# Conditioning dots laid out anew, one section of them moved to the end, and norms from sums and squares

## The chip, the cores and the metric

The kernel runs on one core of a Trainium2 chip. The core has a matrix engine (TensorE, PE in the profile; its weight loads are PEld), three engines for elementwise work (VectorE = DVE, ScalarE = ACT, GpSimd = POOL), a sequencer that mostly issues transfers (SyncE = SP), and 16 DMA engines. Each engine works through its own instructions in order and waits on semaphores for the others. The metric is the device time of one launch in microseconds, as the median of several runs.

## The reference

One layer of a diffusion backbone: 512 latent tokens `x` and 256 context tokens `ctx`, 1024 channels each. Only the latent stream is returned.

```python
mod_x = (jax.nn.silu(c) @ w_ada + b_ada).reshape(bsz, N_MOD, 1, d)      # N_MOD = 9
mod_c = (jax.nn.silu(c_ctx) @ w_ada + b_ada).reshape(N_MOD, 1, d)
...
def ffn_sublayer(h, m, i, w_up, w_down):
    shift, scale, gate = sub_mod(m, i)                                  # m[3i], m[3i+1], m[3i+2]
    y = swiglu(modulate(h, shift, scale), w_up, w_down)
    return post_ln(DEEPNORM_ALPHA * h + 0.5 * gate * y, ln_g[i], ln_b[i])

x = ffn_sublayer(x, mod_x, 0, ffn1_w_in, ffn1_w_out)                    # first network
ctx = ffn_sublayer(ctx, mod_c, 0, ffn1_w_in, ffn1_w_out)
... # projections, neighbourhood attention, gated delta rule, merge
x = ffn_sublayer(x, mod_x, 2, ffn2_w_in, ffn2_w_out)                    # second network
```

`modulate` is a layer norm followed by scale and shift; `post_ln` is a layer norm with gain and bias. The width of both networks is 2816, which is 22 blocks of 128. `mod_x` has nine sections of 1024 values, counted 0 to 8; section 8 is the gate of the second network, section 2 that of the first, and the context needs only sections 0 to 4.

## The kernel before

**Matmuls.** Float32 products are made of three faster ones. Each weight tile of 128x1024 is loaded raw (tags `wr`, `ra`, `rb`, 512 KB), then split: ACT casts the high half `wh` (L137), DVE subtracts to get the low half `wl` (L139). PE multiplies high by high, low by high and high by low (L192 to L194 for the up products and projections, L211 for the down products). The activations are split the same way (`uxh` and `uxl` for x, `uch` and `ucl` for the context, `hx` and `hc` for the hidden blocks). So each weight passes SP (the load), ACT and DVE before PE can use it, and each of these queues is in order.

**Stages up to 600 us.** (1) The x loop, f = 0 to 7: eight of the 22 hidden blocks for the x tokens, one up unit each (512-column matmuls). (2) The c loop, the same eight blocks for the context (256 columns). (3) `t_sums`: DVE forms sums of activation quarters for the next stage while PE runs the down product of these eight blocks. (4) Fourteen `Seven` units, the other 14 blocks for x and context together, in seven products of 384 columns. (5) `bx`, the down product of these 14 for x, four token tiles; (6) `hc`, the same for the context, two tiles; (7) the projections. Between 600 and 1394 us lie the mixers and the second network's up product, and from 1394 us its down product (called dn2 here).

**The evacuation and the norms.** While `bx` ends, `evac1` (L629 to L634) multiplies each finished bank by the gate and adds the residual (`ax`, 512 columns at a time). `finish1` (L636 on) does two layer norms per tile: `post_ln` (L258, L259), then the norm of the following modulate, whose result `y` is made on ACT. The statistics are two `bn_stats` and a `bn_aggr` on DVE, then `rsqrt_eps` (an addition, and a power on POOL, L114). `to_u` then transposes `y` on PE (L148), ACT scales and shifts it into `u32` (L151, one buffer of 1024 columns), and a split gives `uxh` and `uxl`. This runs for x tile by tile inside `hc`, at its steps 0, 2, 5 and 8, and the projections wait for the last tile.

**The conditioning dots.** `w_ada` is held transposed, 72 tiles of 128x1024. A dot (`dot_cols`, L280) is one DVE operation: tile times the broadcast silu row, with the sum of the product as its second output, one column of `colx` (or of `colc` for the context). `ada_gen` (L290 to L304) walks sections 2 to 8, one tile per step: one load on SP, and one dot, or two in sections 2 to 4. `ada_step(n)` takes n steps of it; the steps are spread over the stages by constants: two behind the x loop, one in each of the first six units of the c loop, one per step of `t_sums`, `ADA2` for the Seven units, `ADA3` for `bx`. A few loops take raw buffers for the dots from those of the weights (`raw1`: five in turn); in `bx` there are two of their own.

**What sets the order.** The code is recorded, and a scheduler with its own costs then lays out each engine's order; `issue_after` holds an instruction behind a mark. The order is fixed when the program is built.

Of the kernel before, what the change touches and what calls it, by code (L numbers as in the profile page):

```python
# [58 lines left out]
def body(ctx, tc, I, out, dbg=None):  # L59
# [96 lines left out]
    class Stream:  # L156
# [120 lines left out]
    def dot_cols(tp, raw, crow, col, c):  # L277

        pr = tl(tp, [P, D], "adap")
        V.scalar_tensor_tensor(pr[:], raw[:], 1.0, crow, op0=ALU.mult, op1=ALU.mult, accum_out=col[:, c:c + 1])  # L280
# [104 lines left out]
    ADA2 = (2,) * 10 + (1, 1, 1, 0)  # L385
    ADA3 = (3, 3, 3, 3, 3, 3, 2, 2)
# [74 lines left out]
    ada_step(2)  # L461
# [14 lines left out]
    for f in range(N1):  # L476
        hc.append(h_c())
        ffn_unit(tp, pp, ws.get(), ws.get(), uch, ucl, NCT, *hc[-1])
        ada_step(f < 6)
    rows_out(tp, "fs", 2)  # L480
    accd = tl(dp, [6, P, D], "accd")

    def t_sums(j):
# [3 lines left out]
        ada_step()  # L487
# [133 lines left out]
    for t in range(4):  # L621
        nc.gpsimd.dma_start(accx[t][:], accd[t])
# [6 lines left out]
    def evac1(p, banks, acc, out, g):  # L629
        for d in range(2):  # L630
# [3 lines left out]
            V.tensor_tensor(out[:, sl], h[:], acc[:, sl], ALU.add)  # L634
# [61 lines left out]
    for t in range(4):  # L696
        evac1(lp, bx[t], accx[t], accx[t], gx)
# [1173 lines left out]
```

## Time and profile before

| | |
|---|---|
| median of 3 runs | 1523.51 us (1523.34 to 1525.52) |
| the profiled execution | 1524.35 us, span 1522.6 us, mean granted PE clock 0.984 |
| busy share | PE 95%, DVE 76%, ACT 43%, POOL 14% |
| bytes moved | 248.03 MB, mean 163 GB/s |

The span runs from the first to the last instruction. In a row of the timeline stand start, duration, engine, line, operation, output and inputs, the count, and in brackets the idle time just before with what ended it. In a row of waits stand engine and tile and line, the releaser, total us, times, longest. In a row of groups: busy time and mean ns, then idle time before them and its releasers. In a row of windows: the window, its length, then busy time and count of PE, PEld, DVE, ACT and POOL, the granted PE clock, the DMA share and GB/s.

### The profile page before, as it was taken

To read this page: it belongs to the slowest core of one execution; us is meant where nothing else is said; L and a number is where in the kernel's file an instruction comes from. 1 tells how busy PE (TensorE), PEld (TensorE's weight loads), DVE (VectorE), ACT (ScalarE), POOL (GpSimd) and SP (SyncE) were. 2 spreads that over 40 slices of the span, in tenths; PEclk is the share of its full clock that TensorE was granted. 3 is DMA by queue.
4 is the path that set the end of the run, shared out by engine and by line. 5 is a ranking of instruction groups with operands and counts; after the bars stand their busy time and mean duration, and the time that the engine had idled before them with its cause. 6 is when DMAs were issued, how large, how long until landed. Compare 5 with 4: busy or idle time off the path is not lost.

```text
span 1522.6 us, 23874 instructions
## 1 busy us (share of the span) xinstructions
PE 1442.9 (95%) x9118; PEld 1265.1 (83%) x9118; DVE 1161.1 (76%) x1992; ACT 648.8 (43%) x1067; POOL 209.6 (14%) x251
## 2 busy tenths in 40 slices
PE   6999999999999988999996999989999999999997
PEld 4779879999997776889875777867778999998886
DVE  8768888999977895768777796567669799886426
ACT  5434424434334165546533444266516444444310
POOL 0000000000010020323301001333232022220001
PEclk9999999999999998999998999999999999999999
DMA  9666775445459643222476623274354143233422
GB/s 371 204 234 225 237 250 208 163 161 200 161 214 344 235 161 119 91 90 85 145 216 171 192 79 122 70 253 139 100 177 139 65 135 111 94 111 139 138 84 83
DMA packets 114756, 248.03 MB, mean 163 GB/s; under 512 B 35073, under 2 KB 50513, under 8 KB 114641
## 3 DMA queue, kind: packets, MB, share of 16 engines
q1 hardware_dynamic: 109632, 227.30, 44.5%
q0 software_dynamic: 3424, 13.90, 2.4%
q10 hardware_dynamic: 1586, 5.32, 0.9%
q8 instruction: 71, 1.16, 0.3%
q14 instruction: 43, 0.35, 0.1%
HBM read 214.98 MB, written 31.50 MB: 162 GB/s over the span
## 4 chain that ended last, share of the span: by engine, by line
PE 65%; DVE 13%; DMA 12%; issue 4%; ACT 3%; POOL 2%; SPq 1%; DVEq 0%; ACTq 0%; POOLq 0%
PE ps L211 12%; PE ps L531 4%; PE ps L530 4%; PE ps L532 4%; PE pm L192 4%; PE pm L193 4%; PE pm L194 4%; PE ps L1659 3%; PE ps L1658 3%; PE ps L1660 3%; DVE wl L139 3%; DMA wr<-in_w_adaT_dram 3%; PE ps L194 3%; PE ps L193 3%; PE ps L192 3%
## 5 line engine op out<-in xcount | busy, mean ns | idle before, releaser
L139 DVE TENSOR_TENSOR wl<-wr,wh 128x1024 fp32r<-128x1024 f32 (+1 forms) x183 | 224.0, 1228 | 115.2 <-ACT wh L137 114.8
L137 ACT CAST wh<-wr 128x1024 fp32r<-128x1024 f32 (+1 forms) x183 | 184.4, 1012 | 292.8 <-PE pm L193 60.3
L192 PE MATMUL pm<-uxh,wh 128*128 128x512 f32 x320 | 132.7, 415 | 1.1 <-ACT spill L777 1.0
L194 PE MATMUL pm<-uxh,wl 128*128 128x512 f32 x320 | 126.9, 397 | 0.7 <-DVE wl L139 0.7
L193 PE MATMUL pm<-uxl,wh 128*128 128x512 f32 x320 | 126.9, 397 | 0.0
L280 DVE SCALAR_TENSOR_TENSOR adap<-wr,crow 128x1024 f32<-128x1024 f32 x92 | 112.1, 1219 | 13.9 <-DMA wr<-in_w_adaT_dram 13.2
L211 PE MATMUL ps<-wh,hx 128*128 128x512 f32 x352 | 97.3, 395 | 4.1 <-ACT wh L137 4.1
L114 POOL TENSOR_TENSOR rs<-ve,mhalf 128x1 f32<-128x1 f32 (+2 forms) x46 | 51.2, 1118 | 327.5 <-DVE ve L110 326.2
L211 PEld LDWEIGHTS ps<-wh,hx 128*128 128x128 f32 x352 | 66.7, 190 | 18.8 <-ACT wh L137 5.0
L194 PEld LDWEIGHTS pm<-uxh,wl 128*128 128x128 f32 x320 | 61.0, 191 | 14.7 <-DVE wl L139 1.6
L192 PEld LDWEIGHTS pm<-uxh,wh 128*128 128x128 f32 x320 | 61.2, 191 | 12.9 <-ACT spill L777 1.9
L192 PE MATMUL ps<-uh,wh 128*128 128x256 f32 (+1 forms) x208 | 68.6, 330 | 2.0 <-ACT wh L137 2.0
L194 PE MATMUL ps<-uh,wl 128*128 128x256 f32 (+1 forms) x208 | 67.6, 327 | 3.0 <-DVE wl L139 3.0
L193 PEld LDWEIGHTS pm<-uxl,wh 128*128 128x128 f32 x320 | 61.4, 192 | 10.5
L192 PE MATMUL ps<-uxh,wh 128*128 128x256 f32 (+1 forms) x192 | 60.6, 324 | 9.6 <-ACT uxh L137 9.6
L193 PE MATMUL ps<-ul,wh 128*128 128x256 f32 (+1 forms) x208 | 67.7, 326 | 0.0
L137 ACT CAST wh<-ra 128x1024 fp32r<-128x1024 f32 x32 | 33.7, 1052 | 75.1 <-issue 16.9
L193 PE MATMUL ps<-uxl,wh 128*128 128x256 f32 (+1 forms) x192 | 61.1, 320 | 1.0 <-DVE uxl L139 0.9
L194 PE MATMUL ps<-uxh,wl 128*128 128x256 f32 (+1 forms) x192 | 60.6, 318 | 0.0
L530 PE MATMUL ps<-ur,wh 128*128 128x384 f32 x168 | 56.5, 336 | 0.0
L531 PE MATMUL ps<-ur,wh 128*128 128x384 f32 x168 | 56.4, 336 | 0.0
L530 PE MATMUL ps<-uh,wh 128*128 128x384 f32 x168 | 56.4, 336 | 0.0
(483 smaller groups left out, 4217.3 us busy)
## 6 DMA issues: line engine op xcount, KB each, us to landing
wr<-in_w_adaT_dram SPq DMA_DIRECT2D x72, 512.0 KB, 4.6
wr<-in_up_dram SPq DMA_DIRECT2D x54, 512.0 KB, 3.4
wr<-in_dn_dram SPq DMA_DIRECT2D x52, 512.0 KB, 3.5
wr<-in_win_dram SPq DMA_DIRECT2D x52, 512.0 KB, 3.5
ra<-in_up_dram SPq DMA_DIRECT2D x26, 512.0 KB, 4.1
rb<-in_up_dram SPq DMA_DIRECT2D x18, 512.0 KB, 3.3
ra<-in_w_adaT_dram SPq DMA_DIRECT2D x16, 512.0 KB, 4.4
wr<-in_w_o_dram SPq DMA_DIRECT2D x8, 512.0 KB, 4.0
```

Of the source, the lines that this page charges most:

```text
L114: G.tensor_tensor(rs[:], ve[:], mhalf[:, 0:n], ALU.pow)
L137: S.copy(hi, src)
L139: marks["lo"] = V.tensor_tensor(lo, src, hi.bitcast(F32), ALU.subtract).ins
L192: T.matmul(ps, a, uh[:, k, :], start=(k == 0), stop=False)
L193: T.matmul(ps, a, ul[:, k, :], start=False, stop=False)
L194: marks["mm"] = T.matmul(ps, b, uh[:, k, :], start=False, stop=(k == nk - 1)).ins
L211: T.matmul(banks[t][d][:, c0:c1], a[:, sl], b[:, d * 512 + c0:d * 512 + c1], start=first and j == 0, stop=last and j == 2)
L280: V.scalar_tensor_tensor(pr[:], raw[:], 1.0, crow, op0=ALU.mult, op1=ALU.mult, accum_out=col[:, c:c + 1])
L530: T.matmul(ps[:], a, mh, start=k == 0, stop=False)
L531: T.matmul(ps[:], a, ml, start=False, stop=False)
L532: T.matmul(ps[:], b, mh, start=False, stop=k == 3)
L1658: T.matmul(ps[:], a, uh[:, k], start=k == 0, stop=False)
```

## The change

It does three things. First, section 8 leaves `ada_gen` (48 steps are left of 56): its eight loads and dots stand in dn2, one at each of the steps j = 5 to 12, in place in the raw tile; the silu row is written to DRAM at the start (`sild`) and broadcast back at j = 4 (`arow`); at j = 13 bias and factor 0.5 are put on, and POOL's queue writes the gate (1024 single values) and broadcasts it into `gx`, which was loaded at dn2's start before. Second, the remaining steps are dealt out anew: the x loop takes six instead of two, the c loop two instead of six, `t_sums` none in its first four steps, Seven 25 instead of 23, `bx` what is left (13 of 19); dots of sections 5 to 7 write in place, `bx` has four raw buffers for dots, and the four `ax` loads go from POOL's queue ahead of `bx` to SP's queue at its steps 4 to 7. Third, in the first network's norms the evacuation's add also gives the sum (`accum_out`), the second affine operation too, and the variance comes from a Square with bias on ACT that sums; POOL does the scaling and the power. `bn_stats` and `bn_aggr` are gone there.

```diff
-    def dot_cols(tp, raw, crow, col, c):
+    def dot_cols(tp, raw, crow, col, c, alone=False):
-        pr = tl(tp, [P, D], "adap")
+        pr = raw if alone else tl(tp, [P, D], "adap")
...
-        for sec in range(2, 9):
+        for sec in range(2, 8):
...
-    ADA2 = (2,) * 10 + (1, 1, 1, 0)
-    ADA3 = (3, 3, 3, 3, 3, 3, 2, 2)
+    ADA2 = (2, 1, 2, 1, 2, 1, 2, 2, 2, 2, 2, 2, 2, 2)
+    ADA3 = (2, 2, 2, 2, 2, 2, 2, 2)
...
     for f in range(F0, N1):
...
-    ada_step(2)
+        ada_step(1 + (f == N1 - 1))
...
     for f in range(N1):
-        ada_step(f < 6)
+        ada_step(f in (0, 2))
+    sild = tl(dp, [1, D], "sild")
+    nc.gpsimd.dma_start(sild[:], crow[0:1, 0])
     def t_sums(j):
-        ada_step()
+        else:
+            ada_step()
...
-    for t in range(4):
-        nc.gpsimd.dma_start(accx[t][:], accd[t])
...
     def evac1(p, banks, acc, out, g):
+        out_sum, nm = tl(p, [P, 2], "os", 6), tl(p, [P, 1], "nm", 6)
         for d in range(2):
             V.tensor_tensor(h[:], banks[d][:], g[:, sl], ALU.mult)
-            V.tensor_tensor(out[:, sl], h[:], acc[:, sl], ALU.add)
+            V.scalar_tensor_tensor(out[:, sl], h[:], 1.0, acc[:, sl], op0=ALU.mult, op1=ALU.add, accum_out=out_sum[:, d:d + 1])
+        V.tensor_scalar(nm[:], out_sum[:, 0:1], out_sum[:, 1:2], -1.0 / D, op0=ALU.add, op1=ALU.mult)
+        return nm
+    def spread(p, src, nm):
+        sq = tl(p, [P, D], "sq")
+        ss = tl(p, [P, 1], "ss", 4)
+        S.activation(sq[:], src[:], AF.Square, bias=nm[:, 0:1], accum_out=ss[:, 0:1])
+        return rsqrt_eps(p, ss[:, 0:1], 1, 1.0 / D)
-    def finish1(p, kind, t, h):
-        post_ln(p, h, lng, lnb)
+    def finish1(p, kind, t, h, nm):
+        rs = spread(p, h, nm)
+        V.scalar_tensor_tensor(h[:], h[:], nm[:, 0:1], lng[:], op0=ALU.add, op1=ALU.mult)
+        s = tl(p, [P, 1], "s1", 4)
+        V.scalar_tensor_tensor(h[:], h[:], rs[:, 0:1], lnb[:], op0=ALU.mult, op1=ALU.add, accum_out=s[:, 0:1])
+        nm = tl(p, [P, 1], "nm", 4)
+        V.tensor_scalar(nm[:], s[:], -1.0 / D, None, op0=ALU.mult)
+        rs = spread(p, h, nm)
+        V.tensor_tensor(nb[:], nm[:], rs[:], ALU.mult)
-        ln_norm(p, y[:], h, act=True)
+        S.activation(y[:], h[:], AF.Identity, bias=nb[:, 0:1], scale=rs[:, 0:1])
...
     def h_next(j):
+        if j > 3:
+            with tc.issue_after(marks["raw"]):
+                nc.sync.dma_start(accx[j - 4][:], accd[j - 4])
         ada_step(ADA3[j])
-    ada_tp[0], ada_raw[0] = ad, lambda: tl(ad, [P, D], "wr", 2)
+    ada_tp[0], ada_raw[0] = ad, lambda: tl(ad, [P, D], "wr", 4)
...
     gx = tl(lp, [P, D], "gx")
-    bcast_row(gx, gates[(0, 8)])
+    arow = tl(lp, [P, D], "arow")
     def between(j):
+        if j == 4:
+            nc.sync.dma_start(arow[:], sild.broadcast_to([P, D]))
+        if 4 < j < 13:
+            c = 59 + j
+            raw8 = tl(lp, [P, D], "x2", 2)
+            with tc.issue_after(marks["raw"]):
+                nc.sync.dma_start(raw8[:], I["w_adaT"][c])
+            dot_cols(lp, raw8, arow[:], colx, c, True)
+        if j == 13:
+            V.tensor_tensor(colx[:, 64:72], colx[:, 64:72], bcol[:, 64:72], ALU.add)
+            V.tensor_scalar(colx[:, 64:72], colx[:, 64:72], 0.5, None, op0=ALU.mult)
+            nc.gpsimd.dma_start(gates[(0, 8)].rearrange("k p -> p k"), colx[:, 64:72])
+            nc.gpsimd.dma_start(gx[:], gates[(0, 8)].rearrange("k p -> (k p)")[None].broadcast_to([P, D]))
```

The built programs show how the orders move. A row is line, operation, output, input and shape of the output; numbers in names tell tiles apart and differ between the two programs. First DVE at the passage from the x loop to the c loop, before (`hx` and `hc` are the hidden blocks, `fs` the gated product, L280 the dots):

```order
L280 SCALAR_TENSOR_TENSOR adap_1046,colx_72<-wr_1044,crow_83 128x1024
L273 TENSOR_TENSOR fs_1117<-fs_1117,ps_1068 128x256
L280 SCALAR_TENSOR_TENSOR adap_1048,colc_73<-wr_1044,crow_83 128x1024
L139 TENSOR_TENSOR hc_1054<-fs_1117,hc_1054 128x256
L280 SCALAR_TENSOR_TENSOR adap_1124,colx_72<-wr_1122,crow_83 128x1024
L139 TENSOR_TENSOR wl_1132<-wr_1129,wh_1131 128x1024
L280 SCALAR_TENSOR_TENSOR adap_1126,colc_73<-wr_1122,crow_83 128x1024
L139 TENSOR_TENSOR wl_1138<-wr_1135,wh_1137 128x1024
```

And in the change:

```order
L280 SCALAR_TENSOR_TENSOR adap_990,colx_72<-wr_988,crow_83 128x1024
L280 SCALAR_TENSOR_TENSOR adap_992,colc_73<-wr_988,crow_83 128x1024
L273 TENSOR_TENSOR fs_1057<-fs_1057,ps_1008 128x512
L139 TENSOR_TENSOR hx_994<-fs_1057,hx_994 128x512
L280 SCALAR_TENSOR_TENSOR adap_1064,colx_72<-wr_1062,crow_83 128x1024
L139 TENSOR_TENSOR wl_1082<-wr_1079,wh_1081 128x1024
L280 SCALAR_TENSOR_TENSOR adap_1066,colc_73<-wr_1062,crow_83 128x1024
L139 TENSOR_TENSOR wl_1088<-ra_1085,wh_1087 128x1024
L280 SCALAR_TENSOR_TENSOR adap_1070,colx_72<-wr_1068,crow_83 128x1024
L273 TENSOR_TENSOR fs_1141<-fs_1141,ps_1092 128x256
L280 SCALAR_TENSOR_TENSOR adap_1072,colc_73<-wr_1068,crow_83 128x1024
L139 TENSOR_TENSOR wl_1162<-wr_1159,wh_1161 128x1024
```

The dots, which stood around the c loop's second unit (`wl_1132`, `wl_1138`), now stand around its first one (`wl_1082`, `wl_1088`), and `wl_1162`, the second up half of the second unit, comes before the first.

Second, ACT's casts at the end of `t_sums`, before, where `wh_1902` and `wh_1938` belong to the down product that PE runs there and the others to later weights:

```order
L137 CAST ur_1852<-ur_98 128x384
L137 CAST ur_1855<-ur_98 128x384
L137 CAST wh_2056<-ra_2054 128x1024
L137 CAST wh_1902<-wr_1900 128x1024
L137 CAST wh_1938<-wr_1936 128x1024
```

And in the change:

```order
L137 CAST ur_1836<-ur_98 128x384
L137 CAST ur_1839<-ur_98 128x384
L137 CAST wh_1880<-wr_1878 128x1024
L137 CAST wh_1916<-ra_1914 128x1024
L137 CAST wh_2034<-ra_2032 128x1024
```

The later weight's cast now stands behind the two that the down product needs.

Third, ACT at the beginning of `hc`, before (`wh_4872` is the first weight that `hc` needs behind those it has from `bx`):

```order
L137 CAST wh_4878<-wr_4876 128x1024
L137 CAST wh_4872<-wr_4870 128x1024
L243 ACTIVATE h_870_4778<-ps_4779 8x128
L243 ACTIVATE h_872_4783<-ps_4784 8x128
L644 DMA x1d_4108<-ax_733_4092 128x1024
L137 CAST wh_4944<-wr_4942 128x1024
L137 CAST wh_4962<-wr_4960 128x1024
L137 CAST wh_4980<-wr_4978 128x1024
L130 ACTIVATE y_885_4821<-ax_733_4092,nb_4831,rs_889_4829 128x1024
```

And in the change, where `wh_4823` is that weight:

```order
L137 CAST wh_4829<-wr_4827 128x1024
L644 ACTIVATE sq_4762,ss_4763<-ax_719_4075,nm_4700 128x1024
L663 DMA x1d_4087<-ax_719_4075 128x1024
L644 ACTIVATE sq_4774,ss_4775<-ax_719_4075,nm_4772 128x1024
L137 CAST wh_4823<-wr_4821 128x1024
L644 ACTIVATE sq_4845,ss_4846<-ax_720_4076,nm_4709 128x1024
L137 CAST wh_4894<-wr_4892 128x1024
L243 ACTIVATE h_839_4735<-ps_4736 8x128
L660 ACTIVATE y_859_4783<-ax_719_4075,nb_4781,rs_857_4779 128x1024
L137 CAST wh_4912<-wr_4910 128x1024
```

Both Squares of tile 0 now stand ahead of that cast, and the Square of tile 1 and the `y` of tile 0 ahead of the next ones.

More of the change, by code (lines that the diff above doesn't have):

```diff
@@ L173, in fill @@
                 raw = self.raw() if self.raw else tl(rp, [P, D], "wr", rb)
-                nc.sync.dma_start(raw[:, 0:c], src)
+                marks["raw"] = nc.sync.dma_start(raw[:, 0:c], src).ins
                 hi = tl(p, [P, D], "wh", bufs, F32R)
@@ L242, in to_row @@
         T.transpose(ps[:], cols, ident)
-        S.activation(t, ps[:], AF.Copy, scale=0.5)
-        nc.sync.dma_start(row, t)
+        S.activation(t[:], ps[:], AF.Copy, scale=0.5)
+        nc.sync.dma_start(row, t[:])
     def bcast_row(dst, row):
@@ L298, in ada_gen @@
                     for w, col in which:
-                        dot_cols(tps[0], raw, crow[:, w], col, sec * 8 + k)
+                        dot_cols(tps[0], raw, crow[:, w], col, sec * 8 + k, sec > 4)
                 if k < KT - 1:
@@ L633, in evac1 @@
             V.tensor_tensor(h[:], banks[d][:], g[:, sl], ALU.mult)
-            V.tensor_tensor(out[:, sl], h[:], acc[:, sl], ALU.add)
-    def finish1(p, kind, t, h):
-        post_ln(p, h, lng, lnb)
+            V.scalar_tensor_tensor(out[:, sl], h[:], 1.0, acc[:, sl], op0=ALU.mult, op1=ALU.add, accum_out=out_sum[:, d:d + 1])
[11 more added lines that the diff above has]
+        V.scalar_tensor_tensor(h[:], h[:], rs[:, 0:1], lnb[:], op0=ALU.mult, op1=ALU.add, accum_out=s[:, 0:1])
         if f"x1{kind}" in dbg:
             nc.sync.dma_start(dbg[f"x1{kind}"][t * P:(t + 1) * P, :], h[:])
+        nm = tl(p, [P, 1], "nm", 4)
+        V.tensor_scalar(nm[:], s[:], -1.0 / D, None, op0=ALU.mult)
+        rs = spread(p, h, nm)
+        nb = tl(p, [P, 1], "nb", 4)
+        V.tensor_tensor(nb[:], nm[:], rs[:], ALU.mult)
         y = tl(p, [P, D], "y1", 2)
-        ln_norm(p, y[:], h, act=True)
+        S.activation(y[:], h[:], AF.Identity, bias=nb[:, 0:1], scale=rs[:, 0:1])
         if kind == "x":
@@ L695, in body @@
     lng, lnb = load_ln(fc, 0)
-    for t in range(4):
-        evac1(lp, bx[t], accx[t], accx[t], gx)
+    nms = [evac1(lp, bx[t], accx[t], accx[t], gx) for t in range(4)]
     rows_out(lp, "h1", 2)
@@ L707, in between @@
             t = FIN1.index(j)
-            u2(fc, pp, "x", t, finish1(fc, "x", t, accx[t]))
+            u2(fc, pp, "x", t, finish1(fc, "x", t, accx[t], nms[t]))
     def after(t, j, banks):
         if j == NT - 1:
-            evac1(lp, banks, x1c[t], x1c[t], gc)
+            nms.append(evac1(lp, banks, x1c[t], x1c[t], gc))
     FIN1 = (0, 2, 5, 8)
@@ L985, in body @@
         if m > 1:
-            ys.append(finish1(fc, "c", len(ys), x1c[len(ys)]))
+            ys.append(finish1(fc, "c", len(ys), x1c[len(ys)], nms[4 + len(ys)]))
     units = []
```

## The prediction

> **What bounds the kernel now.** I read the page's busy times first, then what TensorE (PE) waited for, then the busy times by stage, and last the orders of the single stages around each wait.
>
> ```profile
> span 1522.6 us, 23874 instructions
> PE 1442.9 (95%) x9118; PEld 1265.1 (83%) x9118; DVE 1161.1 (76%) x1992; ACT 648.8 (43%) x1067; POOL 209.6 (14%) x251
> ...
> PE ps L192 <- ACT uxh L137: 9.6, 1, 9.6
> PE ps L211 <- ACT wh L137: 4.1, 2, 2.1
> PE ps L194 <- DVE wl L139: 3.0, 3, 1.6
> PE ps L192 <- ACT wh L137: 2.0, 3, 1.1
> PE ps L211 <- DVE wl L139: 1.9, 2, 1.2
> ```
>
> PE is busy 95% of the span: the change can only win what PE stands idle or runs slowly, and lose by making it stand longer. The rows after "..." are PE's waits (total, times, longest) that lie in the stages the change touches: 20.6 us. Next the stages, one row each: window, length, then busy time and count of PE, PEld, DVE, ACT, POOL, then PE's granted clock, the DMA share and GB/s.
>
> ```profile
> 54.00:122.00 68.00, 65.76 (x301) 52.73 (x300) 48.28 (x85) 28.86 (x47) 0.00 (x0) 1.00 0.66 217
> 122.00:172.00 50.00, 47.25 (x374) 46.02 (x373) 41.59 (x65) 21.37 (x32) 0.00 (x0) 0.97 0.73 242
> 172.00:205.00 33.00, 30.96 (x137) 25.32 (x135) 31.70 (x57) 13.49 (x24) 0.00 (x0) 1.00 0.69 232
> 240.00:440.00 200.00, 200.00 (x1152) 200.00 (x1151) 189.87 (x301) 78.94 (x105) 8.09 (x15) 1.00 0.49 169
> 440.00:516.00 76.00, 73.95 (x332) 61.58 (x331) 52.30 (x80) 23.13 (x34) 3.71 (x7) 1.00 0.91 323
> 516.00:567.00 51.00, 48.81 (x229) 39.72 (x229) 48.92 (x85) 25.02 (x44) 10.91 (x9) 1.00 0.52 180
> 567.00:581.00 14.00, 4.28 (x13) 2.80 (x12) 12.92 (x24) 8.48 (x16) 2.27 (x11) 0.63 0.29 97
> 1394.00:1490.00 96.00, 96.00 (x425) 79.42 (x425) 36.79 (x40) 30.42 (x38) 0.00 (x0) 1.00 0.36 126
> ```
>
> In order: x loop, c loop, t_sums with its down product, the Seven units, the first network's down product for x (bx), for the context (hc), the hole at its end, the second network's down product. DVE is full in four of them (31.70 of 33 us, 189.87 of 200, 48.92 of 51, 12.92 of 14); in the last it is busy 36.79 of 96. PE's order of instructions is the same in both kernels from 600 us on, and so are the others' except for the added dots. So seven stages can move, and I price each.
>
> **The prices of the parts.**
>
> ```profile
> L280 DVE SCALAR_TENSOR_TENSOR adap<-wr,crow 128x1024 f32<-128x1024 f32 x92 | 112.1, 1219 | 13.9 <-DMA wr<-in_w_adaT_dram 13.2
> L139 DVE TENSOR_TENSOR wl<-wr,wh 128x1024 fp32r<-128x1024 f32 (+1 forms) x183 | 224.0, 1228 | 115.2 <-ACT wh L137 114.8
> L119 DVE BATCH_NORM_STATS2 bst<-ax 128x6 f32<-128x512 f32 x8 | 5.5, 684 | 0.0
> L634 DVE TENSOR_TENSOR ax<-h,ax 128x512 f32<-128x512 f32 x6 | 4.0, 682 | 0.0
> L114 POOL TENSOR_TENSOR rs<-ve,mhalf 128x1 f32<-128x1 f32 x11 | 12.7, 1169 | 109.1 <-DVE ve L110 109.1
> L110 POOL TENSOR_SCALAR ve<-ss x12: 228/670/1547, 620.3 to 733.8; 128x4 f32<-128x4 f32 x8, 128x2 f32<-128x2 f32 x4
> L906 ACT ACTIVATE sq<-pg x12: 383/598/611, 618.5 to 731.1; 128x512 f32<-128x512 f32 x8, 128x256 f32<-128x256 f32 x4
> L1420 ACT ACTIVATION_READ_ACCUMULATOR pr<-sc,nm x32: 192/203/220, 994.7 to 1083.6; 128x1 f32 x32
> ```
>
> A dot takes 1.22 us of DVE (with the read of its sum about 1.3). Norms: 24 bn_stats of 0.68 us leave DVE, 16.3 us; the add in the evacuation becomes an add with a sum. No row has that form at 512 columns; the bounds are the plain add, 0.68, and a whole dot, 1.3, and I take 0.75, since the dot costs no more than a plain 1024-column operation beside it (1219 against 1228 ns) and its sum's read 0.08. What comes in on other engines per tile: two Squares of 1024 columns on ACT, 1.4 us each by twice the 0.60 of 512 columns and 0.20 for the sum (bounds 1.2 and 1.6), and twice a POOL pair of 0.67 and 1.17 us, where before DVE did the small operation.
>
> **x loop and c loop, 54 to 172.** The rows are windows of the c loop.
>
> ```profile
> 122.00:127.00 5.00, 5.00 (x45) 5.00 (x44) 4.93 (x9) 0.79 (x2) 0.00 (x0) 1.00 0.58 202
> 127.00:132.00 5.00, 3.13 (x18) 2.72 (x18) 4.59 (x9) 2.83 (x4) 0.00 (x0) 0.82 0.48 152
> 132.00:137.00 5.00, 5.00 (x38) 5.00 (x38) 2.41 (x4) 1.63 (x3) 0.00 (x0) 0.84 0.92 313
> 157.00:162.00 5.00, 4.12 (x32) 3.69 (x31) 3.86 (x5) 3.45 (x6) 0.00 (x0) 1.00 0.67 232
> ```
>
> At full pace 45 matmuls of 256 columns fit in 5 us; 27, 7 and 13 are missing, 47 of 0.111 us: 5.2 us lost. The x loop loses 68.00 less 65.76, 2.2. In total 7.4. The change puts four more steps (eight dots, four loads of 512 KB) into the x loop and takes four out of the c loop. DVE idles 19.7 us in the x loop and would take 10.4 more; DMA goes from 217 GB/s by 2.1 MB in 68 us to about 250, of the 323 moved in bx. So the x loop can hold them. At its end, however, the shown order puts six dots among the c loop's first weight halves, and the second weight of the second c unit ahead of that unit's first; followed by hand with the durations above, PE stands 1.3 and then 4.4 us there, after which the c loop is nearly without dots. With the x loop's 2.2 left, 7.9 against 7.4: I call it **0**. Bounds: -5.2 (the c loop's loss gone), +6 (the same stall again with the x loop's 2.2 tripled).
>
> **t_sums, 172 to 240.**
>
> ```profile
> 202.35 0.61 PE L211 MATMUL ps<-wh,hx 128*128 128x512 f32 x2
> 205.04 3.57 PE L211 MATMUL ps<-wh,hx 128*128 128x512 f32 x8 [2.08 <-ACT wh L137]
> 208.41 0.79 PE L211 MATMUL ps<-wl,hx 128*128 128x512 f32 x2
> ...
> 203.00 1.04 ACT L137 CAST wh<-ra 128x1024 fp32r<-128x1024 f32 x1 [7.01 <-PE ps L211]
> 203.95 1.04 ACT L137 CAST wh<-wr 128x1024 fp32r<-128x1024 f32 x1
> ```
>
> The cast at 203.00 is of a later weight, and waits for PE itself; the cast PE needs stands behind it and ends at 204.99. After the hole 8 matmuls take 3.37 us instead of 1.81 (at 96.00 us / 425 = 0.226 each, as in the last window above), so 2.1 + 1.6 = 3.7 are lost. In the new order the two needed casts come first, and six of DVE's dots are gone from this stage. I take **-3.5**; bounds -3.7 and 0.
>
> **Seven, 205 to 440.** 39 dots instead of 33: DVE 189.87 + 7.8 = 197.7 of 200 us. PE loses nothing there now, though the first five units hold four dots each; the new table spreads them, three in each of the first six. **0**, bounds 0 and +4 (half of the 7.8 in units where DVE is already full).
>
> **bx, 440 to 516.**
>
> ```profile
> 462.42 2.11 PE L211 MATMUL ps<-wh,hx 128*128 128x512 f32 x8 [2.05 <-ACT wh L137]
> ...
> 461.32 1.04 ACT L137 CAST wh<-wr 128x1024 fp32r<-128x1024 f32 x1 [2.19 <-DMA wr<-in_dn_dram]
> ```
>
> A weight's transfer is late while the DMA engines are full (share 0.91 over the stage). Six conditioning loads (3 MB) leave, and the four accumulator tiles (2 MB) come after it instead of just ahead: **-2.0**, bounds -2.3 and +2 (the tiles, now on SP's queue among the weights, delay a later one).
>
> **hc and the hole, 516 to 581.**
>
> ```profile
> 530.77 0.73 PE L211 MATMUL ps<-wl,hc 128*128 128x512 f32 x2 [1.17 <-DVE wl L139]
> ...
> 566.37 1.03 PE L148 MATMUL ps<-ident,y 128*128 128x128 f32 x8
> 577.04 1.65 PE L192 MATMUL ps<-uxh,wh 128*128 128x512 f32 x3 [9.64 <-ACT uxh L137]
> 580.94 0.40 PE L192 MATMUL ps<-uxh,wh 128*128 128x512 f32 x1
> ...
> 573.59 2.90 ACT L151 ACTIVATE u<-ps,colx 128x128 f32<-128x128 f32 x8 [4.65 <-DVE uxl L139]
> ```
>
> Lost now: 1.9 on weight halves (first fence), 9.6 in the hole, and 2.1 behind it (eight matmuls from 577.04 to 580.94, which at 0.226 take 1.8): 13.6. The hole is tile 3's norm: its u operations wait for the one u32 buffer, which DVE frees late.
>
> In the new order, counted from tile 0's last bank: PE has 52 matmuls in hand, 11.8 us. DVE evacuates tile 0 (2.7), ACT squares (to 4.3), POOL (to 6.1); DVE reaches the second affine operation at 8.2, ends it at 9.5, and two adds of tile 2 stand ahead of the mean, 11.1. ACT squares again to 12.5 and only then casts the weight that PE wants at 11.8, ready 13.6: **1.8** lost. Its low half stands on DVE behind the bias of tile 0, which waits for POOL until 14.4, ready 15.7: **1.3**. The same pattern at tiles 1 and 2, with less ahead of it, gives about **2.5**. At the end tile 3 is transposed 12 matmuls before hc ends instead of behind it; its u operations wait for tile 2's low half, its cast stands behind a Square of the context, and its low half behind one context evacuation: **4.5**. Together 10.1 against 13.6, **-3.5**; bounds -9.5 (chain never late, 4 us at the end) and 0.
>
> That the remaining holes are short is worth something: after 9.64 us PE went on slowly (granted 0.63 over that stage), after 2.05 us at full clock (x8 in 2.11 us), after 2.08 us slowly (x8 in 3.57 us). The Trainium skill ("TensorE: Matmul & The Clock Gate", Part 1) says that the clock halves after an idle window of about 3.4 us and comes back after one of work. By it my shorter holes cost no clock; the 2.08 us hole above disagrees, and by that row two of them would cost 1.6 each and the term be about 0.
>
> **Second network's down product.**
>
> ```profile
> L1751 DVE TENSOR_TENSOR h<-ps,gx x8: 679/688/692, 1489.5 to 1514.2; 128x512 f32<-128x512 f32 x8
> ```
>
> Eight dots and their loads among 22 weights. DVE has 59 us free of 96 and adds 10.4; DMA share is 0.36. The first use of gx is at 1489.5, the last dot some 30 us earlier in the order (a 4 KB write and a broadcast follow on POOL's queue, which is empty there). **0**, bounds 0 and +3. Without that cover each dot would cost its 1.3.
>
> Sum: -3.5 - 2.0 - 3.5 = **-9.0**. The profiled execution took 1524.35 for a span of 1522.6; the new one comes to 1515.35. The median of the runs, 1523.51, is 0.84 below that execution, so I expect **1514.5**.
>
> **Rivals.**
> 1. *The norm chain gains nothing.* ACT and POOL stand in DVE's place and the weight casts queue behind Squares; term 0, total 1518.0. For it: two more engine changes per norm, POOL at 1.17 per power. Against: DVE loses 16 us in a stretch where it is full. The Trainium skill ("Vector Engine (DVE) Microarchitecture Reference", 7) says that this form of operation with two 32-bit sources runs at half speed with a sum; by that each add would cost 0.6 more and the outcome be this one. The dot row, 1219 ns beside 1228, shows no such loss.
> 2. *More is won*: the c loop's 5.2 goes and the hole shrinks to 4. 1514.5 - 5 = 1509.5, or lower. For it: DVE's load falls in every stage that stalled.
> 3. *The x loop stalls once more*: eight dots at the transition, +5, total 1519.5. For it: the waits at 122 to 132 are of just this kind.
> 4. *Slower: the x loop becomes bound by its raw buffers.* Seven loads per unit of 11.7 us turn through five buffers, each held until its dots are done. The wait is seen already (13.2 us of DVE's idle before dots). If the turn takes 2.5 us longer than PE's 11.7 in each of the five units, 12.5 us are lost: 1527. It decides from 2.4 us a unit. Against: 250 GB/s asked, 323 seen.
>
> **How the numbers follow.** Forecast 0.45, rival 1 0.15, rival 2 0.15, rival 3 0.13, rival 4 0.12. Below 0.2% (3 us) this kernel's measurement can't tell a change, so "faster" is below 1520.5, "slower" above 1526.5. Forecast and rival 2 count as faster, of rivals 1 and 3 about half to two thirds, the rest as no change: faster 0.77, same 0.12, slower 0.11. Range: 1506 (part of rival 2 left out) to 1523 (rival 4 left out); the forecast's own is 1511 to 1518.
>
> **What would show it.** Right: the wait near 203 gone; the one near 460 shorter; the hole at 567 at 3 to 6 us, with Square ahead of the cast; waits for wh in hc's first 15 us; windows from 600 to 1490 equal in length. Wrong: the x loop longer than 70 us; a PE wait for wl in the second down product; DVE at 100% with PE below it in Seven.

## The result

The changed kernel takes 1511.34 us (median, 1508.31 to 1513.27) against 1523.42 for the kernel before: 0.9919 of its time, interval 0.9896 to 0.9943. Its profiled execution took 1512.61 us for a span of 1510.8, 11.8 less than the 1522.6 of before. Forecast were 1514.5 and a span 9.0 shorter.

The stages can be read from where their first and last instructions start. Rows of a line's instructions (count, shortest/median/longest duration in ns, first and last start in us, forms), of the kernel before:

```profile
L211 PE MATMUL ps<-wh,hx x352: 388/389/632, 170.0 to 522.2; 128*128 128x512 f32 x176
L211 PE MATMUL ps<-wh,hc x176: 387/389/477, 217.7 to 566.1; 128*128 128x512 f32 x176
L192 PE MATMUL ps<-uxh,wh x192: 278/280/792, 577.0 to 1388.1; 128*128 128x256 f32 x128, 128*128 128x512 f32 x64
L192 PE MATMUL pm<-uxh,wh x320: 387/389/795, 608.1 to 997.7; 128*128 128x512 f32 x160
L211 PE MATMUL ps<-wh,hh x176: 389/389/397, 1394.3 to 1513.3; 128*128 128x512 f32 x176
```

And of the changed kernel:

```profile
span 1510.8 us, 23895 instructions
...
L211 PE MATMUL ps<-wh,hx x352: 387/389/504, 169.2 to 516.8; 128*128 128x512 f32 x176
L211 PE MATMUL ps<-wh,hc x176: 387/389/504, 212.8 to 562.1; 128*128 128x512 f32 x176
L192 PE MATMUL ps<-uxh,wh x192: 276/279/628, 563.9 to 1376.6; 128*128 128x256 f32 x128, 128*128 128x512 f32 x64
L192 PE MATMUL pm<-uxh,wh x320: 387/389/795, 596.6 to 987.2; 128*128 128x512 f32 x160
L211 PE MATMUL ps<-wh,hh x176: 389/389/395, 1382.8 to 1501.8; 128*128 128x512 f32 x176
```

The first `hx` row's first start ends the c loop, the first `hc` start ends the x tiles of the first down product (the t_sums stage), the last `hx` start ends `bx`, the last `hc` start ends `hc`; then come the projections (`ps<-uxh`, and from about 600 us `pm<-uxh`), and `hh` is dn2. Differences of these starts, for all kernels run (us; the last column is the span less the start of dn2):

| kernel | to c loop's end | t_sums | Seven, bx | hc | hole | first projections | 600 to dn2 | dn2, end |
|---|---|---|---|---|---|---|---|---|
| before | 170.0 | 47.7 | 304.5 | 43.9 | 10.9 | 31.1 | 786.2 | 128.3 |
| the change | 169.2 | 43.6 | 304.0 | 45.3 | 1.8 | 32.7 | 786.2 | 128.0 |
| norms_only | 168.5 | 46.9 | 302.8 | 47.2 | 4.2 | 36.2 | 788.0 | 128.3 |
| dots_only | 169.0 | 43.7 | 302.1 | 49.3 | 1.8 | 32.8 | 782.7 | 128.0 |
| u32x2 | 170.1 | 47.6 | 302.2 | 43.9 | 4.6 | 35.0 | 783.2 | 128.3 |
| t_steps | 169.5 | 44.5 | 304.4 | 43.9 | 2.1 | 32.1 | 785.7 | 128.1 |
| ts_only | 169.5 | 43.6 | 304.1 | 59.4 | 4.3 | 32.9 | 790.7 | 128.2 |
| old_xc | 170.2 | 43.6 | 303.9 | 44.8 | 1.8 | 32.6 | 784.2 | 128.1 |
| sec8_bx | 168.4 | 43.7 | 302.7 | 49.0 | 2.0 | 32.3 | 789.5 | 128.5 |
| acc_pool | 170.2 | 43.6 | 306.3 | 42.0 | 4.9 | 32.6 | 777.8 | 128.3 |
| after_again | 170.5 | 43.6 | 303.9 | 45.5 | 1.8 | 32.8 | 787.8 | 128.0 |
| acc_pool5 | 168.7 | 43.6 | 306.2 | 42.0 | 4.4 | 32.0 | 779.4 | 128.3 |
| after_u2 | 169.9 | 43.6 | 304.0 | 46.3 | 3.5 | 32.6 | 784.0 | 128.0 |
| accp_u2 | 169.9 | 43.7 | 306.2 | 42.0 | 4.3 | 32.5 | 778.6 | 128.3 |

So the 11.8 us are: 0.8 before the c loop's end, 4.1 in t_sums, 0.5 in Seven and bx, 6.1 from the end of bx to 600 us (hc, hole and first projections: 85.9 to 79.8), 0.3 in dn2 and the end, and nothing between. The change and after_again are the same kernel; so are acc_pool and acc_pool5. Their rows differ by up to 1.5 in the first column, 0.6 in the next five and 1.6 in the one before the last, so a smaller difference in one profile says nothing. Totals spread more: six executions of after_again on one chip took 1508.31 to 1517.62 us. Hole and first projections have to be read together, since a wait behind the first of the projections' products counts in the latter.

### The profile page after: what moved, and what is told of

It is laid out like the page before. It is cut to its first block, busy times and chain, and to the rows that moved or that the text cites. A ratio compares the mean times of both kernels' runs of the same rounds, so it can differ in the third digit from the quotient of the medians.

```text
span 1510.8 us, 23895 instructions
## 1 busy us (share of the span) xinstructions
PE 1441.6 (95%) x9117; PEld 1262.9 (84%) x9117; DVE 1149.5 (76%) x1975; ACT 662.8 (44%) x1090; POOL 211.2 (14%) x262
## 4 chain that ended last, share of the span: by engine, by line
PE 69%; DVE 13%; DMA 10%; issue 4%; ACT 3%; POOL 1%; SPq 1%; DVEq 0%; ACTq 0%; POOLq 0%
PE ps L211 15%; PE ps L533 4%; PE ps L535 4%; PE ps L534 4%; PE pm L192 4%; PE pm L193 4%; PE pm L194 4%; PE ps L193 3%; PE ps L192 3%; PE ps L1679 3%; PE ps L194 3%; PE ps L1680 3%; PE ps L1681 3%; PE pc L1049 2%; DVE wl L139 2%
## 5 line engine op out<-in xcount | busy, mean ns | idle before, releaser
L280 DVE SCALAR_TENSOR_TENSOR adap<-wr,crow 128x1024 f32<-128x1024 f32 x61 | 74.6, 1223 | 2.3 <-DMA wr<-in_w_adaT_dram 1.7
L137 ACT CAST wh<-ra 128x1024 fp32r<-128x1024 f32 x31 | 32.6, 1053 | 58.1 <-PE ps L534 20.2
```

Source lines behind the costliest of these rows:

```text
L137: S.copy(hi, src)
```

## The profile after

The stages as windows (columns as ahead of the prediction), changed kernel:

```profile
172.00:205.00 33.00, 33.00 (x147) 27.34 (x146) 26.12 (x45) 12.49 (x20) 0.00 (x0) 1.00 0.68 239
240.00:440.00 200.00, 200.00 (x1151) 199.83 (x1150) 190.47 (x301) 78.43 (x104) 7.59 (x14) 1.00 0.48 164
440.00:516.00 76.00, 75.14 (x329) 61.35 (x328) 51.53 (x86) 22.77 (x35) 2.49 (x5) 1.00 0.84 311
516.00:567.00 51.00, 46.10 (x211) 36.05 (x210) 37.34 (x66) 39.07 (x71) 11.45 (x17) 1.00 0.41 147
1383.00:1502.00 119.00, 119.00 (x526) 98.57 (x525) 66.41 (x89) 30.46 (x38) 6.11 (x5) 1.00 0.47 159
```

In the t_sums window PE is busy for all 33 us, and DVE 26.12 instead of 31.70. In Seven PE is full as before, with DVE at 190 of 200. In the 51 us of hc DVE went from 48.92 to 37.34 and ACT from 25.02 to 39.07. In dn2 PE is full with the eight dots beside it.

The end of hc, PE first and then ACT:

```profile
558.63 1.04 PE L148 MATMUL ps<-ident,y 128*128 128x128 f32 x8
561.83 0.62 PE L211 MATMUL ps<-wh,hc 128*128 128x512 f32 x2
563.86 0.73 PE L192 MATMUL ps<-uxh,wh 128*128 128x512 f32 x2 [1.41 <-ACT uxh L137]
564.81 0.50 PE L192 MATMUL ps<-uxh,wh 128*128 128x512 f32 x1 [0.21 <-ACT wh L137]
566.62 0.79 PE L193 MATMUL ps<-uxl,wh 128*128 128x512 f32 x1 [1.31 <-DVE uxl L139]
...
559.27 2.91 ACT L151 ACTIVATE u<-ps,colx 128x128 f32<-128x128 f32 x8 [3.25 <-DVE x1c L636]
562.03 1.19 ACT L644 ACTIVATE sq<-x1c,nm 128x1024 f32<-128x1024 f32 x1
563.16 0.65 ACT L137 CAST uxh<-u 128x512 fp32r<-128x512 f32 x1
```

Tile 3's transposes come 12 matmuls before the end of hc, its u operations start at 559.27, after a wait put down to DVE's queue, and the context's Square stands ahead of its cast, as the order said. The 9.64 us are now 1.41, 0.21 and 1.31.

What the new operations take, and the eight dots in dn2 (groups of the changed kernel's hc, then a row of the dots' line):

```profile
L636 DVE SCALAR_TENSOR_TENSOR ax<-h,ax 128x512 f32<-128x512 f32 x8 | 5.2, 688 | 0.0
L644 ACT ACTIVATE sq<-ax,nm 128x1024 f32<-128x1024 f32 x8 | 9.4, 1170 | 12.1 <-DVE nm L637 6.4 <-DVE nm L655 5.6
L114 POOL TENSOR_TENSOR rs<-ve,mhalf 128x1 f32<-128x1 f32 x12 | 10.2, 848 | 1.0
L112 POOL TENSOR_SCALAR ve<-ss 128x1 f32<-128x1 f32 x12 | 5.5, 454 | 73.6 <-ACT sq L644 73.6
...
L280 DVE SCALAR_TENSOR_TENSOR x<-x,arow x8: 1218/1220/1227, 1403.5 to 1428.8; 128x1024 f32<-128x1024 f32 x8
```

## The experiments

Up to the end of the c loop and in the stretch from 600 us to dn2 the kernels differ by chance and by their order (more on that below); so the stages in the table decide, and total times only where there are several.

### Which part made the hole at 567

**norms_only**: the kernel before with the third part of the change (`evac1`, `spread` and `finish1` as there, and their calls).

```diff
...
-            u2(fc, pp, "x", t, finish1(fc, "x", t, accx[t]))
+            u2(fc, pp, "x", t, finish1(fc, "x", t, accx[t], nms[t]))
```

> The kernel before with the third part alone (sums in the evacuation, Squares on ACT, no bn_stats); every dot stands where it stood before. Theory A (the forecast's: the norms' work on DVE made the hole at 567): the hole falls from 9.6 to 6 us or less although the dots are still among the evacuations, hc and hole together win 2.5 to 4, the t_sums stall at 203 stays at 2.1, total about 1520. Theory B (DVE's load from the dots made it): the hole stays within 1.5 us of 9.6, total 1522 to 1525.

Measured: 1522.78 us, ratio 0.9987 (0.9970 to 1.0004) with 1523.88 for before on the same chip. PE's waits there:

```profile
526.58 0.73 PE L211 MATMUL ps<-wl,hc 128*128 128x512 f32 x2 [1.32 <-DVE wl L139]
549.42 1.09 PE L148 MATMUL ps<-ident,y 128*128 128x128 f32 x8 [1.70 <-ACT y L659]
569.63 1.65 PE L192 MATMUL ps<-uxh,wh 128*128 128x512 f32 x3 [3.81 <-ACT uxh L137]
572.57 0.80 PE L193 MATMUL ps<-uxl,wh 128*128 128x512 f32 x1 [1.30 <-DVE uxl L139]
605.84 0.51 PE L192 MATMUL pm<-uxh,wh 128*128 128x512 f32 x1 [1.86 <-ACT u L151]
```

The hole falls to 3.81 and 1.30, and hc and hole together are 3.4 us shorter, as theory A had it. But hc alone is 3.3 us longer, and the first projections take 5.1 more: 1.30 and 1.86 of it are the last two waits, and the remaining 2.0 us go with the granted clock, which stays at half while PE works:

```profile
573.00:576.00 3.00, 3.00 (x8) 2.33 (x8) 0.52 (x4) 2.69 (x5) 0.87 (x3) 0.50 0.52 158
576.00:579.00 3.00, 3.00 (x9) 2.35 (x9) 2.28 (x2) 0.92 (x1) 2.02 (x11) 0.58 0.43 168
```

From the end of bx to 600 us it takes 87.6 instead of 85.9. The norms alone win nothing.

**dots_only**: the change with the old norms (`evac1` and `finish1` as before, with bn_stats, bn_aggr and plain adds).

```diff
-        nms.append(evac1(lp, banks, x1c[t], x1c[t], gc))
+        evac1(lp, banks, x1c[t], x1c[t], gc)
...
```

> The changed kernel with the old norms (bn_stats and bn_aggr, plain adds): only the dots' layout, the section moved to the end and the accumulator loads are changed. Theory A: t_sums wins 4.1 as in the changed kernel, the hole stays at 8 to 10 us, hc and hole win at most 1.5, total about 1517. Theory B: hc and hole win 5 to 6 as in the changed kernel, total about 1511 to 1513.

Measured: 1513.09 us, ratio 0.9928 (0.9901 to 0.9956). The hole:

```profile
525.00 1.22 PE L211 MATMUL ps<-wl,hc 128*128 128x512 f32 x2 [2.59 <-DVE wl L139]
542.67 0.73 PE L211 MATMUL ps<-wl,hc 128*128 128x512 f32 x2 [0.65 <-DVE wl L139]
546.47 0.73 PE L211 MATMUL ps<-wl,hc 128*128 128x512 f32 x2 [0.76 <-DVE wl L139]
565.91 0.73 PE L192 MATMUL ps<-uxh,wh 128*128 128x512 f32 x2 [1.46 <-ACT uxh L137]
568.69 0.69 PE L193 MATMUL ps<-uxl,wh 128*128 128x512 f32 x1 [1.33 <-DVE uxl L139]
```

The hole closes without the new norms too, so theory A does not hold alone. But DVE, which still has the bn_stats, is now late with weight halves during hc (2.59, 0.65, 0.76), so that hc and hole win 3.7 and not theory B's 5 to 6, and the stretch from the end of bx takes 83.9. With both parts it takes 79.8: 2.0 from the dots alone, minus 1.7 from the norms alone, 6.1 together. The first start of `pm<-uxh`, which ends the first projections, lies at 608.1 before, 605.8 with the norms, 598.7 with the dots, 596.6 with both. So the dots carry 9.4 of the 11.5 us won by then. The 2.1 that the norms add are 4.1 won behind bx less 1.9 lost in Seven and bx, and they are little more than the spread (the change's second profile is there at 598.1). The totals, 0.9928 here and 0.9919 for the change, can't tell the two kernels apart: that the new norms make the whole kernel faster is not shown.

**u32x2**: the kernel before with two u32 buffers for the first network's tiles (`fc_[0]` is their pool).

```diff
-        u32 = tl(tp, [P, KT, P], tag)
+        u32 = tl(tp, [P, KT, P], tag, 2 if tag == "u32" and tp is fc_[0] else 1)
```

> The kernel before with two u32 buffers for the first network's x tiles and nothing else. Theory A1 (the hole is the wait for the one u32 buffer): tile 3's u operations no longer wait 4.65 us for tile 2's low half, the hole falls from 9.6 to about 5, total about 1519. Theory A2 (DVE's queue is late as a whole, and the buffer only shows it): tile 3's low half comes as late as before, the hole loses under 1.5 us, total 1522 to 1524.

```profile
568.43 1.65 PE L194 MATMUL ps<-uxh,wh 128*128 128x512 f32 x3 [3.33 <-ACT uxh L137]
572.53 0.79 PE L195 MATMUL ps<-uxl,wh 128*128 128x512 f32 x1 [2.45 <-DVE uxl L139]
```

Measured, in one execution: 1516.67 us. The hole is 3.33 and 2.45, 5.8 together: theory A1. The stretch from bx to 600 us takes 83.5, 2.4 less than before, and the first projections 3.9 more than there: PE waits 2.45 us for tile 3's low half and then works at half clock until about 578. So the buffer passed the delay on; what is late behind it is DVE. Three different edits (fewer dots, cheaper norms, one more buffer) each take much of the hole away, and each alone gives much of that back nearby.

**sec8_bx**: the change, with the second network's gate back in the early dots.

```diff
-        for sec in range(2, 8):
+        for sec in range(2, 9):
-    ADA3 = (2, 2, 2, 2, 2, 2, 2, 2)
+    ADA3 = (3, 3, 3, 3, 3, 2, 2, 2)
```

> The changed kernel with the second network's gate section back in the early dots: eight loads and dots more by the end of bx, none in dn2. Theory B (dots among bx and the evacuations make the hole): hc and hole together 4 to 6 us longer than in the changed kernel, PE waits of several us for wl or uxh there, dn2 unchanged; total 1514 to 1518. Rival (the new norms alone suffice, once t_sums is freed): hc and hole within 1 us of the changed kernel, total 1511 to 1513.

Measured: hc 49.0 instead of 45.3 and hole 2.0 instead of 1.8, together 3.9 us more than in the change. Theory B's 4 to 6 is nearly met and its rival falls, but the waits are smaller than the several us that were expected:

```profile
522.65 1.19 PE L211 MATMUL ps<-wh,hc 128*128 128x512 f32 x4 [0.51 <-ACT wh L137]
524.79 0.73 PE L211 MATMUL ps<-wl,hc 128*128 128x512 f32 x2 [0.95 <-DVE wl L139]
547.88 1.09 PE L148 MATMUL ps<-ident,y 128*128 128x128 f32 x8 [2.18 <-ACT y L658]
```

From the end of bx to 600 us it takes 83.3, 3.5 more than the change. At 600 us it is 1.5 behind the change, level with the change's second profile (598.1 both) and still 10.0 ahead of the kernel before. So most of what is won by 600 us does not need the move of section 8. Its total (1517.85, a single time) is further off because of the later stretch.

### The stall at 203

**t_steps**: the change, with a conditioning step in all six steps of t_sums.

```diff
-        else:
-            ada_step()
+        ada_step()
```

> The changed kernel with a conditioning step in each of the first four steps of t_sums again (eight dots more there, four steps fewer later); in the resulting order one later weight's cast stands between the two that the down product needs. Theory C (the order of ACT's casts made the stall at 203): PE waits there for ACT's wh again, 1 to 2.5 us, and the t_sums stage gives back 2 to 3.7. Theory D (DVE's dots made it): PE waits for DVE's wl there, 1 to 3 us. If neither is seen, the stage stays as in the changed kernel, within 0.5 us.

```profile
203.01 2.11 PE L211 MATMUL ps<-wh,hx 128*128 128x512 f32 x8 [0.56 <-ACT wh L137]
```

The wait is for ACT's cast, 0.56 us, and the stage is 0.9 longer. Eight more dots on DVE there bring no wait for `wl`, so theory D falls. Theory C has the right wait with less than the size it gave (1 to 2.5 us, and 2 to 3.7 for the stage). Of the 4.1 us won in t_sums the eight dots can account for 0.9 at most.

**ts_only**: the kernel before, with no step in the first four of t_sums. ACT's order there becomes that of the change.

```diff
-        ada_step()
+        if j >= 4:
+            ada_step()
```

> The kernel before with no conditioning step in the first four steps of t_sums (its four steps fall to later stages) and nothing else; the resulting order has the two needed casts ahead of the later weight's. Theory C (the stall at 203 is the order of the casts plus DVE's load there): no wait at 203, the t_sums stage 4 us shorter as in the changed kernel, the hole at 567 at 9 to 10 us as before, since the steps come back later; total 1519 to 1521. Rival: the four steps (six to eight dots) make bx or hc longer by as much, total 1523 or more.

Measured: 1530.14 us, ratio 1.0047 (1.0033 to 1.0061): slower, by 0.5%. t_sums takes 43.6, the full 4.1 us are won, as theory C had it. Its total is missed, as is its hole of 9 to 10 us (4.3), and the rival's total (1523 or more) comes about:

```profile
528.22 0.38 PE L242 MATMUL ps<-ident,colx 128*8 128x128 f32 x1 [10.53 <-DVE colx L303]
539.91 1.22 PE L211 MATMUL ps<-wl,hc 128*128 128x512 f32 x2 [2.89 <-DVE wl L139]
```

The steps left out pile up behind bx, where all that are left are run at once because a gate is due, and PE waits 10.5 us for its bias. It is the pile that costs: in sec8_bx, where `ADA2` and `ADA3` deal the steps out over Seven and bx, t_sums is free without any dot in dn2, and no such wait is seen. In every kernel with the two needed casts in front the stage takes 43.6 or 43.7, in the three with the old order 46.9 to 47.7.

### The x loop and the accumulator loads

**old_xc**: the change, with the x and c loops' steps as before.

```diff
-        ada_step(1 + (f == N1 - 1))
+    ada_step(2)
-        ada_step(f in (0, 2))
+        ada_step(f < 6)
```

> The changed kernel with the x loop's and the c loop's steps dealt as before (two behind the x loop, six in the c loop). Forecast's theory (the two ways cost the same, 7.9 against 7.4 us): the end of the c loop comes within 1 us of the changed kernel's 169.2. Rival (eight dots moved into the x loop avoid stalls): it comes 2 to 5 us later.

Measured: 170.2 at the c loop's end, with 169.2 and 170.5 in the change's two profiles. The two layouts cost the same, as forecast.

**acc_pool**: the change, with the accumulator loads as before.

```diff
-        if j > 3:
-            with tc.issue_after(marks["raw"]):
-                nc.sync.dma_start(accx[j - 4][:], accd[j - 4])
...
+    for t in range(4):
+        nc.gpsimd.dma_start(accx[t][:], accd[t])
```

> The changed kernel with the four accumulator loads on POOL's queue ahead of bx, as before. Theory E (their transfer ahead of bx made the stall at 460): PE waits 1 to 2.5 us for a weight cast near 455 to 465, bx 1 to 2 us longer. Rival (they only changed places with another late weight): bx within 0.6 us of the changed kernel's.

Seven and bx take 306.3 instead of 304.0, with waits of 1.59 near 458 and 1.34 near 471: theory E. But hc is 3.3 us shorter and the hole 3.1 longer, so that 600 us is passed at 599.6; and the total is 1507.45 in one execution, won in the stretch behind 600 us. The next four kernels, timed on one chip, follow this up.

### The stretch that nothing touches

**after_again** is the changed kernel; **acc_pool5** is acc_pool; **after_u2** has two u32 buffers and one y buffer; **accp_u2** has both edits.

```diff
-        u32 = tl(tp, [P, KT, P], tag)
+        u32 = tl(tp, [P, KT, P], tag, 2 if tag == "u32" and tp is fc_[0] else 1)
...
-        y = tl(p, [P, D], "y1", 2)
+        y = tl(p, [P, D], "y1", 1)
```

> The changed kernel itself, beside the next three on one chip, so that they can be compared with it: 1509 to 1513, the start of the projections' second part within 1.5 us of 596.6, the stretch from there to the second network's down product within 2 us of 786.

> The changed kernel with the accumulator loads on POOL's queue ahead of bx, timed. Theory F (another order of the instructions between 600 and 1394 us, which the scheduler happened on, is worth the difference): it reaches 600 us 2 to 3 us later than the changed kernel, is 5 to 9 us shorter in the stretch to the second down product, and its median lies 3 to 5 us below the changed kernel's. Rival (its single look was a lucky execution): its median lies within 1.5 us of the changed kernel's, and the stretch is within 2 us of 786.

> The changed kernel with two u32 buffers and, for room, one y buffer instead of two. Theory A1 (what is left of the hole is still the wait for the u32 buffer): the three waits at the end of hc (2.9 us together) fall to 1.5 or less and the projections begin 1 to 2 us earlier. Rival (with one y buffer the wait moves to the transposes): hc is longer by what the hole loses, within 0.5 us. By theory F its order in the middle stretch is of the shorter kind, and it gains 2 to 4 us there: total 1506 to 1509.

> Both edits together: accumulator loads on POOL's queue, two u32 buffers, one y buffer. The middle stretch as with the loads on POOL's queue (778 to 782), the end of hc as with two u32 buffers: total 1505 to 1508, below both kernels of this case. If the two edits only shift the same waits, it equals the better one of them within 1 us.

Against before on one chip: after_again 1515.16 us, 0.9931 (0.9907 to 0.9955); acc_pool5 1509.10, 0.9895 (0.9873 to 0.9918); after_u2 1511.99, 0.9912 (0.9886 to 0.9938); accp_u2 1508.32, 0.9887 (0.9862 to 0.9912). One stage of the stretch, the attention's transposes and products, in the change and then in acc_pool:

```profile
L1459 PE MATMUL po<-pT,vw x128: 272/273/476, 996.4 to 1077.7; 128*64 128x128 f32 x128
```

```profile
L1458 PE MATMUL po<-pT,vw x128: 272/273/476, 995.9 to 1073.8; 128*64 128x128 f32 x128
```

The same 128 products take 81.3 us in the one and 77.9 in the other. No line of these stages was edited. The scheduler lays them out in another order when something ahead of them changes: ACT's order differs in some 40 places between the two kernels, more than half of them behind 600 us. In the built programs PE's order from 600 us on falls into three groups. Before, the change, norms_only and t_steps share one, with at most one product elsewhere, and their stretch took 785.7 to 788.0. ts_only and sec8_bx share another: 790.7 and 789.5. dots_only, after_u2 and accp_u2 share a third, and u32x2, old_xc and acc_pool come close to it on PE: 777.8 to 784.2. The three ranges do not overlap, so theory F holds for the stretch. The order is not all, though: dots_only, after_u2 and accp_u2 have it in common on PE, DVE and ACT (there but for one instruction) and took 782.7, 784.0 and 778.6; where those 5 us lie was not traced.

acc_pool5's median lies 6.1 us below after_again's, more than theory F's 3 to 5; up to 600 us it was not behind (596.9 against 598.1). after_again itself lies above the 1509 to 1513 expected of it, with its stages as expected. With a second u32 buffer and one y buffer less nothing closed in the change (hole 3.5 instead of 1.8, waits of 3.07 and 0.98): A1 is not borne out there. after_u2's stretch took 784.0, and its total missed the 1506 to 1509 of the expectation. accp_u2 equals acc_pool5 within 0.8 us, as its expectation had it, just above the 1505 to 1508 given. accp_u2 and acc_pool5 lie 6 to 7 us below the change on that chip, and below both kernels of this case; the intervals of accp_u2 and after_again overlap only at 0.9907 to 0.9912.

## Why the prediction was right, and where it was wrong

**x and c loops**, 0 forecast, -0.8 found, of which 0.4 lie ahead of these loops; the change's own two profiles differ by 1.3 here. The stalls at the passage, followed by hand as 1.3 and 4.4 us, are there: PE waits 2.42, 0.22, 0.34 and 1.09 us for ACT's casts between 120 and 136 us, and runs slowly behind the first of these waits:

```profile
122.00:127.00 5.00, 4.04 (x20) 3.75 (x21) 4.28 (x5) 1.91 (x3) 0.00 (x0) 0.66 0.40 118
127.00:132.00 5.00, 4.67 (x39) 4.46 (x39) 4.34 (x8) 2.59 (x4) 0.00 (x0) 1.00 0.88 272
132.00:137.00 5.00, 3.91 (x33) 3.71 (x32) 3.79 (x6) 1.33 (x2) 0.00 (x0) 1.00 0.83 262
137.00:142.00 5.00, 5.00 (x45) 5.00 (x44) 3.36 (x5) 3.39 (x5) 0.00 (x0) 1.00 0.71 247
```

43 matmuls of 135 are missing in the first 15 us, 4.8 us, and then the loop is full. With the 2.6 us that PE idles between 54 and 122 these are 7.4, against 7.9 forecast and 7.4 before. Right, and so rivals 3 and 4 fell.

**t_sums**, -3.5 forecast, -4.1 found. Right, by the mechanism named: the casts' order. ts_only shows the gain without the rest of the change, and t_steps that the dots (eight fewer here, not six as the step has it) bring at most 0.9 of it. What the step left out is where the four steps go: where they pile up behind bx, as in ts_only, they cost more than they bring.

**Seven**, 0: right; PE is full in both windows.

**bx**, -2.0 forecast, at most -0.5 found. Wrong. The step read a 2.05 us wait of one execution as a property of the kernel. norms_only and u32x2 issue the same instructions up to there and have no wait in bx. The change has one at another weight, near 478, of 0.86 us and in its second profile 0.78. So the wait shrank by 1.2 us, and about 0.6 of that was lost again because PE ran more slowly between 495 and 517 us (last section).

**hc and the hole**, -3.5 forecast, -6.1 found. The sign was right, the cause only in part, and the size was off. The cause: the step followed the new norm chain and named no share of the dots. The norms alone lose 1.7 there, the dots' leaving alone wins 2.0, and only the two together win 6.1, because DVE must be ahead both during hc, for the weight halves, and at its end. The size: the waits that were followed by hand were smaller, 0.46 and 0.39 for the first weight instead of 1.8 and 1.3, 1.05 later instead of 2.5 (PE waited for a tile's `y` there, not for a weight), and 2.9 at the end instead of 4.5. The POOL pair, taken as 1.84 us, measured 0.45 + 0.85 = 1.30; the add with a sum measured 0.69 and 0.09 for 0.75; the Square 1.17 and 0.20 for 1.4. Rival 1's condition, that this add runs at half speed as the Trainium skill has it ("Vector Engine (DVE) Microarchitecture Reference", 7), is refuted by the 688 ns, beside 682 for the plain add.

Part of what the smaller waits won went to the clock:

```profile
564.00:567.00 3.00, 1.48 (x4) 0.73 (x5) 3.00 (x7) 1.28 (x2) 0.55 (x1) 0.93 0.00 0
567.00:570.00 3.00, 3.00 (x8) 2.32 (x8) 2.69 (x6) 0.21 (x1) 0.00 (x0) 0.50 0.42 130
570.00:573.00 3.00, 3.00 (x14) 2.44 (x14) 0.82 (x2) 2.97 (x5) 1.34 (x3) 1.00 0.41 144
```

After three waits of 1.41, 0.21 and 1.31 us the granted clock is 0.50 for three microseconds. Eight matmuls take 3.49 us there (566.62 to 570.11) instead of 1.81: 1.7 lost, where the hole before cost 2.1 behind it. The step held that short holes cost no clock, by "TensorE: Matmul & The Clock Gate" of the Trainium skill, Part 1, whose idle window is about 3.4 us; its own row of the 2.08 us hole spoke against that, and the trace sides with the row. Waits and clock come to 6.5 us, where the step had 10.1 for the change and 13.6 for before; of these 7.1 less the stretch shows 6.1, and the rest was not traced. The first projections take 1.6 us longer than before because two of the three waits (0.21 and 1.31) lie in them.

**dn2**, 0: right. The eight dots ran from 1403.5 to 1428.8, 49 us before gx was needed at 1478.0, and PE is full in the window.

**The total** came out 2.8 us lower than the sum: 2.6 too little for hc and the hole, 0.6 for t_sums, 0.8 for the loops and 0.3 for the end, against 1.5 too much for bx. That the sum came this close is partly luck, since two terms were off to opposite sides. At 1511.34 us the change lies at the edge of the forecast's own 1511 to 1518 and nearer to rival 2's 1509.5: of the two things that rival 2 asks for, the hole did shrink below 4 us, and the c loop's loss stayed. Rival 1 falls with the 6.1 us, though what the norms add to the dots is not shown in the total.

## What to carry to other kernels

A wait at the end of a crowded stretch belongs to the whole queue that is late: test it by taking away each of the loads alone, and measure the whole stretch. A second buffer, cheaper norms and fewer dots each took most of the hole away here, and each time part of the delay came back nearby, as waits for other halves or as matmuls at half clock. Moving work off a full stage pays only if it is dealt out to later stages that can hold it; taking four steps out of t_sums won 4.1 us there, and where they piled up PE had to wait 10.5. Where a scheduler orders the program, an edit can change stages that it does not touch, so compare stage by stage and look whether the order behind the edit stayed the same.

## What was not expected of the hardware

Waits of 1.41, 0.21 and 1.31 us within 4.2 us (562.4 to 566.6) were followed by half clock, while a single wait of 2.05 us in bx before was not (eight matmuls in 2.11 us behind it). What decides between them was not tried. In all fourteen profiles the time at half clock behind the hole is close to a multiple of 3.41 us (added up from the granted clock in windows of 0.5 us, 552 to 592 us): none in t_steps, one in the change, after_again, dots_only, sec8_bx, old_xc, acc_pool5 and after_u2, two in ts_only, acc_pool and accp_u2, three in before, norms_only and u32x2. acc_pool and acc_pool5 are the same kernel, so the program alone does not fix the number.

In the change PE ran 3% slower from 494.6 to 517 us without waiting (0.233 us from one matmul's start to the next instead of 0.227), with the granted clock at 1.00; before and change:

```profile
500.00:520.00 20.00, 20.00 (x90) 16.57 (x89) 15.08 (x23) 1.95 (x2) 0.00 (x0) 1.00 0.74 248
```

```profile
500.00:520.00 20.00, 20.00 (x88) 16.04 (x87) 12.01 (x24) 3.35 (x4) 1.98 (x2) 1.00 0.20 72
```

88 matmuls against 90 in the same 20 us. All ten profiles with the new norms show this rate there, and none of the four with the old ones (before, u32x2, ts_only, dots_only). It begins 16 us before the first evacuation (510.4 us), when the new operations are not running yet. Its cause is open.
